# Entry of the MLP: a bank's sum ahead of the next operand's rest, rests of weights sooner, and six sums from VectorE to GpSimd

## The chip, the cores and the metric

One NeuronCore of one Trainium2 chip. The metric is the device time of one execution in microseconds (us). The kernel before took 2927.08 us (median of 3 runs, 2926.19 to 2927.83). TensorE multiplies matrices, VectorE (DVE in the profile), ScalarE (ACT) and GpSimd (POOL) do element-wise work, SyncE (SP) issues most of the DMAs. Each engine executes its own instructions in order and waits on semaphores for the others.

## The reference

One layer of a diffusion transformer, for 256 context tokens and 2048 latent tokens, model width 1024: a modulated RMS norm, one projection, differential attention beside Fourier mixing, an output projection with a gated residual, and then the part that matters here:

```python
xs = xs + g1 * mix
h = rms_norm(xs, norm2_g[l]) * (1 + sc2) + sh2
xs = xs + g2 * sq_relu_mlp(h, w1[l], w2[l])      # square(relu(h @ w1)) @ w2, inner width 4096
```

The same MLP runs for the context tokens `xp`. Everything is float32.

## The kernel before

**Precision.** A float32 product is made of three matmuls on the faster fp32r type. Each operand is split into a high part (ScalarE's cast to fp32r) and a rest (VectorE's `tensor_sub` of operand and high part), and `high*high`, `high*rest` and `rest*high` are summed in PSUM.

**Seven products.** `h @ w1` is done as a 2x2 block product with seven multiplications in place of eight. The 2304 tokens stand in 18 tiles of 128; tile `t` is paired with tile `t + 9`, and the pairs form three token blocks `b` of 384 columns. Seven operands on the token side (`hop[p][b]`, DMAed from a scratch tensor to a tile `hr`, split into `mhh` and `mhl`) meet seven on the weight side. A weight set `q` holds four 128x512 blocks `a11`, `a12`, `a21`, `a22` and four sums of them, `s1` to `s4`; `LEFT` says which one product `p` takes, and its split is `ophW` (high) and `oplW` (rest). Sets 0 to 15 are block 0, and so on.

**The MLP's loop.** `ITEMS` is the order of the products: (q, p) = (0,1), (0,6), (0,2), (0,7), (0,5), (0,4), (1,1), (1,6), (0,3), (1,2), (1,7), (1,5), (1,4), ... The third product of a set stands two places late. One item is 12 matmuls of 128x384 (`mms`, four slices by three parts). Four PSUM banks are used, and products share them: 1 and 2 add up in bank A, 6 and 7 in B, 5 and 3 in C, 4 has D. Between two products of a bank VectorE or ScalarE must read the sum so far: `post` copies A (`us`), makes `u2` and `u3` from B and `us`, and `uz` from C or D. ScalarE turns `uz` into `g` (relu, then square: `squares`), GpSimd sums the `g` (`g_add`), and SyncE stores them.

**Order.** It is written out by hand (`manual_schedule`): the instructions of each engine stand as the Python code issues them. In iteration `n` the loop casts the weights of a later item (`CASTS`, then `n + LEAD + 1`); `w_low` issues the rests of all casts that have none yet; `h_prep` makes high part and rest of a token operand. In the first iterations the token operands of block 0 are still being prepared, in the order 1, 6, 2, 7, 5, 4, 3 (`ORDER`). Their DMA tiles `hr` have three buffers, so the load of operand 7 waits for the rest of operand 1 to be made, 5 for 6, 4 for 2 and 3 for 7.

**The entry.** The out-projection's last tile (17, `LAST`, in two halves `xo17_0` and `xo17_1`) still passes VectorE when the MLP's first operands are prepared: `out_post` multiplies a half's PSUM sum by the gate (`gt`) and adds it to `xo`; `x_store` writes `xo` out. `mlp_ahead` puts the first splits among these steps. The sums of set 0 are made ahead (`w_ahead`; `s4` in `mlp_ahead(2)`, in place in the buffer of `a12`), those of set 1 by `w_add` inside the loop, those of set 2 two items later. Weight blocks have eight buffers (two sets).

Of the kernel before, what the change touches and what calls it, by code (L numbers as in the profile page):

```python
# [41 lines left out]
def body(tc, a, out):  # L42
    nc = tc.nc
    ctx = ExitStack()
    with ctx:
# [1270 lines left out]

        def h_prep(b, p):
            src = HR.pop((b, p))
            pool = hpa if p in (1, 6) else hp[p]
            hi = pool.tile([P, 4, 384], F32R, tag=f"mhh{p}", name=f"mhh{b}_{p}")  # L1320
            lo = pool.tile([P, 4, 384], F32R, tag=f"mhl{p}", name=f"mhl{b}_{p}")
            for c, t in src if isinstance(src, list) else [(slice(0, 4), src)]:
                nc.scalar.copy(hi[:, c, :], t)
                nc.vector.tensor_sub(lo[:, c, :], t, f32(hi[:, c, :]))
            HO[b, p] = hi, lo

        def w_ahead():
# [9 lines left out]
        def mlp_ahead(part):  # L1337

            if part == 0:
                for n in range(2):  # L1340
                    h_prep(0, ORDER[n])
                    w_cast(n)
                    w_low()
                    if n == 0:
                        h_load(0, ORDER[3])
# [14 lines left out]
        with c3o, ExitStack() as c4, ExitStack() as c4x, ExitStack() as c4w:  # L1360
# [67 lines left out]
            def out_post(i, hf):  # L1428
                s = 1 if i < 2 else 0
                gt = t4.tile([P, 512], F32, tag="gt", name=f"gt{i}_{hf}")  # L1430
                nc.vector.tensor_mul(gt, PS.pop((i, hf)), g1[s][:, hf * 512:hf * 512 + 512])
                nc.vector.tensor_add(x_half(i, hf), x_half(i, hf), gt)

# [32 lines left out]
            with tc.manual_schedule():  # L1466
# [42 lines left out]
                for n, i in enumerate(seq[2:], 2):  # L1509
# [6 lines left out]
                    if n == N4 - 1:  # L1516
# [3 lines left out]
                        c5r = ExitStack()  # L1520
                        hpa = c5r.enter_context(tc.tile_pool(name="m_ha", bufs=1, side="right", reuse_waits="tile"))
                    out_post(i, 0)
                    if n == N4 - 1:
                        mlp_ahead(0)
                    finish(seq[n - 1])
# [16 lines left out]
        with c5r, ExitStack() as c5:  # L1542
# [4 lines left out]

            def w_add(q, n):

                R = RAW[q]  # L1550
                x, y, f = (("a21", "a22", nc.vector.tensor_add), ("s1", "a11", nc.vector.tensor_sub),
                           ("a11", "a21", nc.vector.tensor_sub), ("a12", "s2", nc.vector.tensor_sub))[n]
                t = t5.tile([P, 512], F32, tag=f"ws{n}", name=f"ws{n}_{q}", bufs=1)
                f(t, R[x], R[y])
                R[f"s{n + 1}"] = t
# [140 lines left out]
            LAG = []  # L1696
            CASTS = ((), (4,), (5,), (8, 6), (7,), (9,), (10, 11))

            with tc.manual_schedule():
                for n, (q, p) in enumerate(ITEMS):  # L1700
                    b, last = q // NF, q % NF == NF - 1 and q // NF < 2
                    if n < 4:
                        h_prep(0, ORDER[n + 2])
                        if n < 2:
                            h_load(0, ORDER[n + 5])
                    w_low()
                    for c in CASTS[n] if n < len(CASTS) else (n + LEAD + 1,):
                        w_cast(c)
# [5 lines left out]
                    if n == 2:  # L1714
                        mlp_ahead(2)
                    if n == 5:
                        h_prep(0, 3)
                    early = q == 0 and p == 6
                    if early:
                        post(q, p, ps)  # L1720
                    nw = q + 1
                    if q and p == 1 and wset(q) == q:
                        w_add(q, 3)
                    if nw < NQ and wset(nw) == nw:
                        for x in ({7: (0, 1), 5: (2,)} if q == 0 else {6: (0, 1), 2: (2,)}).get(p, ()):
                            w_add(nw, x)
# [235 lines left out]
```

## Time and profile before

| | |
|---|---|
| median of 3 runs | 2927.08 us (2926.19 to 2927.83) |
| the profiled execution, its own time | 2927.01 us |
| its span, first to last instruction | 2925.2 us |
| TensorE busy | 2892.7 us, 99% of the span |
| VectorE, ScalarE, GpSimd busy | 2010.5, 1570.7, 1043.8 us |
| mean granted TensorE clock | 0.998 of full speed |
| MLP's first matmul | 1517.14 us after the span's start |

The timeline views give for each instruction the start, the duration, the engine, the source line, what is written and read, and in brackets how long the engine stood idle before it and who released it. Matmuls are pipelined: each row of 0.34 us starts some 0.17 us after the one before. Buffer numbers are left out of the profile's names, so `mhl` stands for the rest of every token operand and `oplW` for that of every weight operand; the instruction order tells which one it is.

### The profile page before, as it was taken

What the parts mean: (1) busy time and instruction counts of PE and PEld (TensorE: products, weight loads), DVE (VectorE), ACT (ScalarE), POOL (GpSimd) and SP (SyncE); (2) the same over time, 40 slices, a digit from 0 to 9 for tenths busy, and PEclk for the clock granted to TensorE, in tenths of its full rate; (3) what the DMA queues carried; (4) which work ended last, traced back from release to release, by engine and by line L of the source; (5) the groups of instructions that cost most, each with busy time, mean ns of one, the idle gap of its engine ahead of it and who ended that gap; (6) DMA issues with size and microseconds to landing.
All of it is one profiled execution on the core that took longest, in us unless ns stands there. A gap on an engine that the chain in (4) does not pass through costs nothing.

```text
span 2925.2 us, 43918 instructions
## 1 busy us (share of the span) xinstructions
PE 2892.7 (99%) x15497; PEld 2514.0 (86%) x15497; DVE 2010.5 (69%) x3377; ACT 1570.7 (54%) x3535; POOL 1043.8 (36%) x849
## 2 busy tenths in 40 slices
PE   8999999999999999999999999999999999999999
PEld 4888888778888888888889999999998888888887
DVE  6666776788998988974468778777775354345554
ACT  4333323688998989964356556556554322232221
POOL 1111113199898989952213333333332000000000
PEclk9999999999999999999999999999999999999999
DMA  7777878612121211217776667676656454445663
GB/s 279 199 201 190 224 199 260 220 61 76 44 103 43 104 37 44 91 50 214 216 246 208 224 234 235 224 240 221 217 192 229 132 195 150 135 142 176 204 208 108
DMA packets 394414, 495.58 MB, mean 169 GB/s; under 512 B 26403, under 2 KB 307056, under 8 KB 391122
## 3 DMA queue, kind: packets, MB, share of 16 engines
q1 hardware_dynamic: 386560, 477.63, 51.7%
q0 software_dynamic: 2992, 7.28, 0.8%
q10 hardware_dynamic: 4642, 7.88, 0.8%
q8 instruction: 122, 2.00, 0.3%
q14 instruction: 98, 0.80, 0.1%
HBM read 315.20 MB, written 179.57 MB: 169 GB/s over the span
## 4 chain that ended last, share of the span: by engine, by line
PE 93%; ACT 2%; DVE 2%; DMA 1%; POOL 1%; issue 1%; SPq 0%; ACTq 0%; DVEq 0%; POOLq 0%
PE Ss L935 10%; PE ps L87 8%; PE ps L88 8%; PE ps L89 8%; PE pj L88 5%; PE pj L87 5%; PE pj L89 5%; PE pts L990 5%; PE po L87 4%; PE po L89 4%; PE po L88 4%; PE pC L1584 2%; PE pB L1582 2%; PE pB L1584 2%; PE pB L1583 2%; PE pC L1582 2%
## 5 line engine op out<-in xcount | busy, mean ns | idle before, releaser
L940 DVE TENSOR_REDUCE mxs<-Ss 128x1 f32<-128x512 f32 x636 | 413.4, 685 | 66.2 <-PE Ss L935 54.0
L1275 DVE TENSOR_TENSOR sl<-sr,sh 128x768 fp32r<-128x768 f32 x168 | 161.8, 964 | 339.9 <-ACT sh L1274 339.4
L975 POOL TENSOR_TENSOR P0s<-P0s,P1s 128x1024 f32<-128x1024 f32 (+2 forms) x128 | 377.1, 2946 | 10.7
L1274 ACT CAST sh<-sr 128x768 fp32r<-128x768 f32 x168 | 140.2, 835 | 424.9 <-PE ps L88 421.3
L1624 POOL TENSOR_TENSOR gs<-g,g 128x384 f32<-128x384 f32 x48 | 69.7, 1452 | 472.2 <-ACT g L1594 418.2
L959 ACT ACTIVATE P1s<-Ss,mxs 128x512 f32<-128x512 f32 x318 | 215.4, 694 | 36.2 <-DVE mxs L943 34.8
L87 PE MATMUL pj<-wh,hh 128*128 128x512 f32 x576 | 229.4, 398 | 0.7 <-ACT fo L381 0.7
L88 PE MATMUL ps<-tlT,sh 128*128 128x512 f32 x585 | 229.3, 392 | 0.0
L87 PE MATMUL ps<-thT,sh 128*128 128x512 f32 x585 | 229.2, 392 | 0.0
L88 PE MATMUL pj<-wl,hh 128*128 128x512 f32 x576 | 227.9, 396 | 0.5 <-DVE wl L503 0.5
L89 PE MATMUL ps<-thT,sl 128*128 128x512 f32 x585 | 227.7, 389 | 0.0
L89 PE MATMUL pj<-wh,hl 128*128 128x512 f32 x576 | 226.5, 394 | 0.0
L959 ACT ACTIVATE P0s<-Ss,mxs 128x512 f32<-128x512 f32 x318 | 214.3, 691 | 4.6 <-DVE mxs L943 4.0
L935 PE MATMUL Ss<-KS1s,Qs 128*128 128x512 f32 x636 | 196.2, 420 | 5.5 <-ACT P0s L959 3.1
L935 PE MATMUL Ss<-KS0s,Qs 128*128 128x512 f32 x636 | 196.5, 421 | 2.6 <-ACT P1s L959 2.4
L990 PEld LDWEIGHTS pts<-ident,P0s 128*128 128x128 f32 x1280 | 158.3, 140 | 43.0 <-ACT ahs L997 3.3
L990 PE MATMUL pts<-ident,P0s 128*128 128x128 f32 x1280 | 191.3, 273 | 0.7 <-ACT P1s L959 0.7
L1593 ACT ACTIVATE g<-uz 128x384 f32<-128x384 f32 x144 | 75.9, 527 | 203.1 <-DVE uz L1616 172.9
L974 POOL TENSOR_SCALAR P1s<-P1s,tots 128x1024 f32<-128x1024 f32 (+2 forms) x128 | 172.2, 1345 | 5.8
L1002 DVE TENSOR_TENSOR als<-pts,ahs 128x512 fp32r<-128x512 f32 x256 | 165.9, 681 | 6.8 <-ACT ahs L997 6.6
L87 PE MATMUL ps<-ophT,sh 128*128 128x512 f32 x423 | 165.9, 392 | 1.1 <-DVE uz L1616 1.1
L89 PE MATMUL ps<-ophT,sl 128*128 128x512 f32 x423 | 165.7, 392 | 0.0
(622 smaller groups left out, 8230.1 us busy)
## 6 DMA issues: line engine op xcount, KB each, us to landing
sr<-sd SPq DMA_DIRECT2D x84, 768.0 KB, 4.6
a<-in_w SPq DMA_DIRECT2D x184, 256.0 KB, 3.9
sd<-gs SPq DMA_DIRECT2D x192, 192.0 KB, 2.0
sd<-g SPq DMA_DIRECT2D x144, 192.0 KB, 4.4
wm<-in_w_mod SPq DMA_DIRECT2D x32, 512.0 KB, 5.7
Qs<-qd SPq DMA_DIRECT2D x32, 512.0 KB, 3.6
b<-in_w SPq DMA_DIRECT2D x64, 256.0 KB, 5.2
b<-tsum SPq DMA_DIRECT2D x64, 256.0 KB, 4.8
```

The costliest lines, as they stand in the source:

```text
L87: nc.tensor.matmul(ps, lh, rh, start=first, stop=False)
L88: nc.tensor.matmul(ps, lh, rl, start=False, stop=False)
L89: nc.tensor.matmul(ps, ll, rh, start=False, stop=last)
L935: nc.tensor.matmul(S[:, :w], self.Q[:, x, m, j * P:j * P + P], self.hd.KS[m][:, b * 512:b * 512 + w], start=(x == 0), stop=(x == 1))
L940: nc.vector.tensor_reduce(self.mx[j][:, m, b:b + 1], self.S[j, m, b], axis=AX.X, op=ALU.max)
L959: nc.scalar.activation(dst, S, AF.Exp, bias=self.mx[j][:, m, 6:7], accum_out=self.sm[j][:, m, b:b + 1])
L974: nc.gpsimd.tensor_scalar(p, p, tot[:, 3:4], 0.0, op0=ALU.mult, op1=ALU.add)
L975: nc.gpsimd.tensor_add(d, d, p)
L990: nc.tensor.transpose(pt[:, c:c + P], self.p0[j][:, (kb + t) * P:(kb + t + 1) * P], ident)
L1002: nc.vector.tensor_sub(t, self.pt[kb], f32(self.A[kb][0]))
L1274: nc.scalar.copy(hi, src)
L1275: nc.vector.tensor_sub(lo, src, f32(hi))
```

## The change

`mlp_ahead(0)` is split: the first token operand's split is issued before `out_post` of tile 17's first half, the rest of that step after it. Both residual adds of tile 17 (`xo17_0`, `xo17_1`) go from VectorE to GpSimd. `h_prep` becomes `h_parts`, which returns the high part and the rest as two steps; in iteration 1 the rest of operand 7 is issued after `post` of product 6, and with it the load of operand 3. From iteration 2 on, `w_low` runs before the token operand's rest as well. `CASTS` issues the cast for product 3 of set 0 in iteration 5 in place of 3, and `s4` of set 0 is made in iteration 5 in place of 2. All four weight sums of set 1 go to GpSimd, issued in iteration 2 (three of them) and 6 (the fourth). TensorE's and SyncE's orders stay as they are.

```diff
--- before.py
+++ after.py
@@ -1315,14 +1315,27 @@
                 HR[b, p].append((slice(2 * n, 2 * n + 2), f32(t)))
 
         def h_prep(b, p):
+            for half in h_parts(b, p):
+                half()
+
+        def h_parts(b, p):
+
             src = HR.pop((b, p))
             pool = hpa if p in (1, 6) else hp[p]
             hi = pool.tile([P, 4, 384], F32R, tag=f"mhh{p}", name=f"mhh{b}_{p}")
             lo = pool.tile([P, 4, 384], F32R, tag=f"mhl{p}", name=f"mhl{b}_{p}")
-            for c, t in src if isinstance(src, list) else [(slice(0, 4), src)]:
-                nc.scalar.copy(hi[:, c, :], t)
-                nc.vector.tensor_sub(lo[:, c, :], t, f32(hi[:, c, :]))
             HO[b, p] = hi, lo
+            src = src if isinstance(src, list) else [(slice(0, 4), src)]
+
+            def high():
+                for c, t in src:
+                    nc.scalar.copy(hi[:, c, :], t)
+
+            def rest():
+                for c, t in src:
+                    nc.vector.tensor_sub(lo[:, c, :], t, f32(hi[:, c, :]))
+
+            return high, rest
 
         def w_ahead():
 
@@ -1337,8 +1350,11 @@
         def mlp_ahead(part):
 
             if part == 0:
+                h_prep(0, ORDER[0])
+            elif part == 3:
                 for n in range(2):
-                    h_prep(0, ORDER[n])
+                    if n:
+                        h_prep(0, ORDER[n])
                     w_cast(n)
                     w_low()
                     if n == 0:
@@ -1429,7 +1445,7 @@
                 s = 1 if i < 2 else 0
                 gt = t4.tile([P, 512], F32, tag="gt", name=f"gt{i}_{hf}")
                 nc.vector.tensor_mul(gt, PS.pop((i, hf)), g1[s][:, hf * 512:hf * 512 + 512])
-                nc.vector.tensor_add(x_half(i, hf), x_half(i, hf), gt)
+                (nc.gpsimd if i == LAST else nc.vector).tensor_add(x_half(i, hf), x_half(i, hf), gt)
 
             def x_store(i):
                 if i == LAST:
@@ -1519,9 +1535,11 @@
                         ms2 = ctx.enter_context(tc.tile_pool(name="m_s2", bufs=2, side="right", reuse_waits="tile"))
                         c5r = ExitStack()
                         hpa = c5r.enter_context(tc.tile_pool(name="m_ha", bufs=1, side="right", reuse_waits="tile"))
+                    if n == N4 - 1:
+                        mlp_ahead(0)
                     out_post(i, 0)
                     if n == N4 - 1:
-                        mlp_ahead(0)
+                        mlp_ahead(3)
                     finish(seq[n - 1])
                     out_mm(i, 1)
                     if n == N4 - 1:
@@ -1545,11 +1563,12 @@
             pp = c5.enter_context(tc.tile_pool(name="m_p", bufs=2, space=PSUM, reuse_waits="tile"))
             PSB, U, G = {}, {}, {}
 
-            def w_add(q, n):
+            def w_add(q, n, gp=False):
 
                 R = RAW[q]
-                x, y, f = (("a21", "a22", nc.vector.tensor_add), ("s1", "a11", nc.vector.tensor_sub),
-                           ("a11", "a21", nc.vector.tensor_sub), ("a12", "s2", nc.vector.tensor_sub))[n]
+                e = nc.gpsimd if gp else nc.vector
+                x, y, f = (("a21", "a22", e.tensor_add), ("s1", "a11", e.tensor_sub),
+                           ("a11", "a21", e.tensor_sub), ("a12", "s2", e.tensor_sub))[n]
                 t = t5.tile([P, 512], F32, tag=f"ws{n}", name=f"ws{n}_{q}", bufs=1)
                 f(t, R[x], R[y])
                 R[f"s{n + 1}"] = t
@@ -1694,16 +1713,24 @@
 
 
             LAG = []
-            CASTS = ((), (4,), (5,), (8, 6), (7,), (9,), (10, 11))
+            CASTS = ((), (4,), (5,), (6,), (7,), (8, 9), (10, 11))
 
             with tc.manual_schedule():
                 for n, (q, p) in enumerate(ITEMS):
                     b, last = q // NF, q % NF == NF - 1 and q // NF < 2
+                    if n > 1:
+                        w_low()
+                    rest = None
                     if n < 4:
-                        h_prep(0, ORDER[n + 2])
-                        if n < 2:
+                        high, rest = h_parts(0, ORDER[n + 2])
+                        high()
+                        if n != 1:
+                            rest()
+                        if n < 1:
                             h_load(0, ORDER[n + 5])
                     w_low()
+                    if n == 5:
+                        mlp_ahead(2)
                     for c in CASTS[n] if n < len(CASTS) else (n + LEAD + 1,):
                         w_cast(c)
                     squares()
@@ -1712,17 +1739,20 @@
                     if fn:
                         fn(*args)
                     if n == 2:
-                        mlp_ahead(2)
+                        for x in range(3):
+                            w_add(1, x, True)
                     if n == 5:
                         h_prep(0, 3)
                     early = q == 0 and p == 6
                     if early:
                         post(q, p, ps)
+                        rest()
+                        h_load(0, ORDER[6])
                     nw = q + 1
                     if q and p == 1 and wset(q) == q:
-                        w_add(q, 3)
-                    if nw < NQ and wset(nw) == nw:
-                        for x in ({7: (0, 1), 5: (2,)} if q == 0 else {6: (0, 1), 2: (2,)}).get(p, ()):
+                        w_add(q, 3, q == 1)
+                    if q and nw < NQ and wset(nw) == nw:
+                        for x in {6: (0, 1), 2: (2,)}.get(p, ()):
                             w_add(nw, x)
                     if p == (7 if q else 5) and q + 2 < NQ and wset(q + 2) == q + 2:
                         w_load(q + 2)
```

What stands in the engines' orders at three places. First VectorE from the gating of tile 17's second half (`gt17_1`) to the rest of token operand 4 (`mhl0_4`); `mhl0_p` is the rest of token operand p of block 0, `oplW0_p` that of the weight operand of product p in set 0, `u2_0` the sum that reads bank B after product 6. Before:

```order
L1431 TENSOR_TENSOR gt17_1_17333<-po4_17_1_17300,g1_0_15293 128x512
L1432 TENSOR_TENSOR xo17_1_17042<-xo17_1_17042,gt17_1_17333 128x512
L1324 TENSOR_TENSOR mhl0_2_17370<-hr0_2_17001,mhh0_2_17369 128x1536
L1306 TENSOR_TENSOR oplW0_2_17328<-a12_0_16664,ophW0_2_17327 128x512
L1306 TENSOR_TENSOR oplW0_7_17331<-a21_0_16666,ophW0_7_17330 128x512
L1324 TENSOR_TENSOR mhl0_7_17393<-hr0_7_17269,mhh0_7_17392 128x1536
L1606 TENSOR_TENSOR u2_0_17414<-pB0_17401,us_0_17390 128x384
L1324 TENSOR_TENSOR mhl0_5_17417<-hr0_5_17325,mhh0_5_17416 128x1536
L1306 TENSOR_TENSOR oplW0_5_17399<-wsa1_17104,ophW0_5_17398 128x512
L1352 TENSOR_TENSOR a12_0_16664<-a12_0_16664,wsa2_17105 128x512
L1324 TENSOR_TENSOR mhl0_4_17438<-hr0_4_17373,mhh0_4_17437 128x1536
L1306 TENSOR_TENSOR oplW0_4_17422<-a22_0_16668,ophW0_4_17421 128x512
```

With the change:

```order
L1447 TENSOR_TENSOR gt17_1_17333<-po4_17_1_17300,g1_0_15293 128x512
L1336 TENSOR_TENSOR mhl0_2_17370<-hr0_2_17001,mhh0_2_17369 128x1536
L1306 TENSOR_TENSOR oplW0_2_17328<-a12_0_16664,ophW0_2_17327 128x512
L1306 TENSOR_TENSOR oplW0_7_17331<-a21_0_16666,ophW0_7_17330 128x512
L1625 TENSOR_TENSOR u2_0_17411<-pB0_17398,us_0_17390 128x384
L1336 TENSOR_TENSOR mhl0_7_17393<-hr0_7_17269,mhh0_7_17392 128x1536
L1306 TENSOR_TENSOR oplW0_5_17396<-wsa1_17104,ophW0_5_17395 128x512
L1336 TENSOR_TENSOR mhl0_5_17418<-hr0_5_17325,mhh0_5_17417 128x1536
L1306 TENSOR_TENSOR oplW0_4_17422<-a22_0_16668,ophW0_4_17421 128x512
L1336 TENSOR_TENSOR mhl0_4_17444<-hr0_4_17373,mhh0_4_17443 128x1536
```

The add `xo17_1` and the sum into `a12_0` (that is `s4`) are gone from here, `u2_0` stands ahead of `mhl0_7`, and `oplW0_4`, `oplW0_5` ahead of the token rests `mhl0_4`, `mhl0_5`.

Second GpSimd, from the last norm's power (`nrsb8`) to the first sum of `g`. Before:

```order
L84 TENSOR_TENSOR nrsb8_17222<-nssb8_17219,mhalf_178 128x1
L1624 TENSOR_TENSOR gs0_0_17621<-g12_0_17601,g22_0_17503 128x384
L84 TENSOR_TENSOR fss_15268<-fss_15268,mhalf_178 128x1
L1626 TENSOR_TENSOR gs1_0_17655<-gs0_0_17621,g11_0_17448 128x384
L1628 TENSOR_TENSOR gs2_0_17676<-g11_0_17448,g12_0_17601 128x384
```

With the change (`ws0_1` to `ws3_1` are the four weight sums of set 1):

```order
L84 TENSOR_TENSOR nrsb8_17222<-nssb8_17219,mhalf_178 128x1
L1448 TENSOR_TENSOR xo17_0_17041<-xo17_0_17041,gt17_0_17262 128x512
L1448 TENSOR_TENSOR xo17_1_17042<-xo17_1_17042,gt17_1_17333 128x512
L1573 TENSOR_TENSOR ws0_1_17436<-a21_1_17113,a22_1_17115 128x512
L1573 TENSOR_TENSOR ws1_1_17438<-ws0_1_17436,a11_1_17109 128x512
L1573 TENSOR_TENSOR ws2_1_17440<-a11_1_17109,a21_1_17113 128x512
L1573 TENSOR_TENSOR ws3_1_17548<-a12_1_17111,ws1_1_17438 128x512
L1643 TENSOR_TENSOR gs0_0_17621<-g12_0_17601,g22_0_17502 128x384
```

Six 128x512 adds now stand between the two, where nothing stood.

Third ScalarE, from the high part of token operand 4 (`mhh0_4`) to that of operand 3 (`mhh0_3`); `ophW0_3` is the high part of the weight operand for product 3, a cast of `s4`. Before:

```order
L1323 CAST mhh0_4_17437<-hr0_4_17373 128x1536
L1300 CAST ophW0_3_17442<-a12_0_16664 128x512
L1300 CAST ophW1_1_17445<-a11_1_17109 128x512
L1593 ACTIVATE g11_0_17448<-pA0_17377 128x384
L1594 ACTIVATE g11_0_17448<-g11_0_17448 128x384
L1300 CAST ophW1_6_17471<-ws1_1_17465 128x512
L1300 CAST ophW1_2_17500<-a12_1_17111 128x512
L1593 ACTIVATE g22_0_17503<-uz_0_17497 128x384
L1594 ACTIVATE g22_0_17503<-g22_0_17503 128x384
L1323 CAST mhh0_3_17519<-hr0_3_17396 128x1536
```

With the change:

```order
L1332 CAST mhh0_4_17443<-hr0_4_17373 128x1536
L1300 CAST ophW1_1_17447<-a11_1_17109 128x512
L1612 ACTIVATE g11_0_17450<-pA0_17377 128x384
L1613 ACTIVATE g11_0_17450<-g11_0_17450 128x384
L1300 CAST ophW1_6_17468<-ws1_1_17438 128x512
L1300 CAST ophW0_3_17496<-a12_0_16664 128x512
L1300 CAST ophW1_2_17499<-a12_1_17111 128x512
L1612 ACTIVATE g22_0_17502<-uz_0_17492 128x384
L1613 ACTIVATE g22_0_17502<-g22_0_17502 128x384
L1332 CAST mhh0_3_17518<-hr0_3_17414 128x1536
```

`ophW0_3` has moved behind `ophW1_6` and stands just ahead of `ophW1_2`, the two passes on `g22_0` and `mhh0_3`; on VectorE its rest `oplW0_3` now comes after `mhl0_3` and the `uz` of product 4 (before, it came ahead of both).

## Rows read from the trace of the kernel before

**Rows 1.** The page: engine, busy us (share of the span), instructions.

```profile
PE 2892.7 (99%) x15497; PEld 2514.0 (86%) x15497; DVE 2010.5 (69%) x3377; ACT 1570.7 (54%) x3535; POOL 1043.8 (36%) x849
```

**Rows 2.** Busy time by stretch: stretch, length, busy (instructions) per engine, PEclk, DMA share, GB/s.

```profile
1517.10:1545.00 27.90, 24.51 (x133) 22.57 (x132) 24.98 (x33) 17.28 (x27) 0.00 (x0) 1.00 0.66 224
...
1600.00:1700.00 100.00, 100.00 (x578) 100.00 (x577) 76.48 (x122) 57.94 (x112) 34.41 (x28) 1.00 0.68 222
```

**Rows 3.** TensorE in order of time at the MLP entry: start us, us, instruction, [idle before].

```profile
1517.14 0.34 PE L1582 MATMUL pA<-mhh,ophW 128*128 128x384 f32 x1
...
1524.42 0.41 PE L1582 MATMUL pB<-mhh,ophW 128*128 128x384 f32 x1 [0.85 <-ACT ophW L1300]
...
1532.77 0.44 PE L1584 MATMUL pA<-mhh,oplW 128*128 128x384 f32 x1 [0.65 <-DVE oplW L1306]
...
1538.12 0.44 PE L1583 MATMUL pC<-mhl,ophW 128*128 128x384 f32 x1 [1.07 <-DVE mhl L1324]
1538.40 0.34 PE L1584 MATMUL pC<-mhh,oplW 128*128 128x384 f32 x1
...
1542.91 0.44 PE L1582 MATMUL pB<-mhh,ophW 128*128 128x384 f32 x1 [0.50 <-DVE u L1606]
```

**Rows 4.** VectorE in order of time, same stretch, same columns.

```profile
1517.34 0.69 DVE L1431 TENSOR_TENSOR gt<-po,g 128x512 f32<-128x512 f32 x1 [0.41 <-PE po L89]
1518.06 0.69 DVE L1432 TENSOR_TENSOR xo<-xo,gt 128x512 f32<-128x512 f32 x1
1518.67 1.75 DVE L1324 TENSOR_TENSOR mhl<-hr,mhh 128x1536 fp32r<-128x1536 f32 x1
1520.34 1.29 DVE L1306 TENSOR_TENSOR oplW<-a,ophW 128x512 fp32r<-128x512 f32 x2
1522.05 1.76 DVE L1324 TENSOR_TENSOR mhl<-hr,mhh 128x1536 fp32r<-128x1536 f32 x1 [0.42 <-ACT mhh L1323]
1523.72 0.55 DVE L1606 TENSOR_TENSOR u<-pB,us 128x384 f32<-128x384 f32 x1
...
1527.36 1.76 DVE L1324 TENSOR_TENSOR mhl<-hr,mhh 128x1536 fp32r<-128x1536 f32 x1 [0.21 <-ACT mhh L1323]
...
1542.31 0.55 DVE L1606 TENSOR_TENSOR u<-pB,us 128x384 f32<-128x384 f32 x1
```

**Rows 5.** ScalarE in order of time, same stretch, same columns.

```profile
1520.54 1.48 ACT L1323 CAST mhh<-hr 128x1536 fp32r<-128x1536 f32 x1 [0.61 <-DVE mhl L1324]
...
1534.81 1.46 ACT L1323 CAST mhh<-hr 128x1536 fp32r<-128x1536 f32 x1
```

**Rows 6.** The chain that ended last, in order of time: start us, us, what.

```profile
1520.45 5.37 DMA hr<-hd
```

**Rows 7.** VectorE and GpSimd, last tiles of the out-projection, in order of time.

```profile
1502.33 1.07 DVE L1432 TENSOR_TENSOR xo<-xo,gt 128x512 f32<-128x512 f32 x1
...
1502.92 1.62 POOL L1460 TENSOR_TENSOR ht<-hTb,ht 128x512 f32<-128x512 f32 x1
```

**Rows 8.** VectorE and GpSimd, change of token block inside the MLP, in order of time.

```profile
1749.74 1.76 DVE L1324 TENSOR_TENSOR mhl<-hr,mhh 128x1536 fp32r<-128x1536 f32 x1 [0.85 <-ACT mhh L1323]
...
1749.84 2.53 POOL L1626 TENSOR_TENSOR gs<-gs,g 128x384 f32<-128x384 f32 x1
...
1751.88 1.04 DVE L1306 TENSOR_TENSOR oplW<-ws,ophW 128x512 fp32r<-128x512 f32 x1
...
1752.34 1.47 POOL L1628 TENSOR_TENSOR gs<-g,g 128x384 f32<-128x384 f32 x1
...
1753.38 2.05 DVE L1324 TENSOR_TENSOR mhl<-hr,mhh 128x1536 fp32r<-128x1536 f32 x1
```

**Rows 9.** TensorE near the start of the kernel, in order of time.

```profile
37.91 1.33 PE L494 MATMUL pta<-ident,x 128*128 128x128 f32 x5 [2.18 <-DVE hTa L479]
```

**Rows 10.** Busy time by stretch near the start, columns as in rows 2.

```profile
38.00:39.00 1.00, 1.00 (x5) 1.00 (x6) 0.96 (x2) 1.00 (x3) 0.00 (x0) 0.50 0.49 197
...
44.00:45.00 1.00, 1.00 (x5) 0.87 (x4) 1.00 (x3) 1.00 (x3) 0.00 (x0) 0.87 0.91 279
```

## The prediction

> **What bounds the kernel now.** I read the page first: TensorE is busy 99% of the span [rows 1], so the change can pay only where TensorE waits, and next the windows by stage. From 1600 to 1700 us TensorE is never idle and begins 578 matmuls in 100 us, one per 0.173 us; from 1517.1 to 1545 us, the MLP's entry, it is busy 24.51 of 27.90 us [rows 2]. The timeline of TensorE shows the waits there: for the high part of an operand (and, by the program, for the sum that reads bank B), for a weight's rest, for a token's rest, for `u` [rows 3]; three shorter ones stand between. Between 1517.14 and 1542.91 lie ten items of 12 matmuls, 120 x 0.173 = 20.8 us of work in 25.8 us: 5.0 us are lost, 0.17% of the kernel. That is the most that could be won here.
>
> Who is late? VectorE is busy 24.98 of the 27.90 us [rows 2], and its timeline explains each wait [rows 4]. `u2_0` (bank B) could have run at 1521.5, when product 6 ended, but stands behind the rest of operand 7 and ends at 1524.27; TensorE begins product 7 at 1524.42. The rest of operand 4 ends at 1529.12, and from there to the third matmul of product 3 at 1538.40 VectorE and ScalarE pass work to each other without a long pause: 9.3 us. `u2_1` ends at 1542.86, product 7 of set 1 begins at 1542.91. So VectorE sets the entry's pace.
>
> **The change part by part, without GpSimd's side.** The token rests cost VectorE 1.67 us from start to next start (1522.05 to 1523.72), the 512-wide rests 0.60 (two in 1.29, the second overlapping the first), `u` 0.47 [rows 4].
>
> The first operand's rest ahead of `gt17_0`, and `xo17_0` taken off, lie before 1517.34, where VectorE waits 0.41 us for TensorE anyway [rows 4]: worth nothing to TensorE. (GpSimd's `xo17_0` may hold operand 6's rest by a turn, worked out below at 1.1 us; the step then ends near 1517.0, still inside that wait. Without this cover `gt17_1` would be late by what is over.) Operand 7's load starts some 1.7 us sooner, but nothing below waits for it.
>
> From `gt17_1` on, in the new order: operand 2's rest needs no `xo17_1` ahead of it and starts at 1517.96, two weight rests follow, VectorE is free at 1520.8. `u2_0` waits for product 6, 1521.53 to 1522.05. Operand 7's high part ends at 1522.02 [rows 5], its rest runs from 1522.05 as before. Then `oplW0_5`, operand 5, `oplW0_4`, operand 4: 0.60 + 1.67 + 0.60 + 1.75 after 1523.72 is 1528.35. Before it was 1529.12 [rows 4]; saved 0.8.
>
> The way from there to product 3's third matmul has new members: `u3_0`, `oplW1_1`, `uz`, `oplW1_6`, `s4` on VectorE (2.8 us), then on ScalarE `ophW0_3`, which now waits for `s4`, and behind it `ophW1_2`, two passes of `g22` and operand 3's high part (3.6 with 1.46 for the last [rows 5]), then operand 3's rest, `uz`, `oplW0_3` on VectorE (2.9): 9.2 us, as long as before. So what TensorE wins ahead of product 3 it loses there, in two waits (operand's rest, then weight's rest) where there was one. Behind it VectorE has four instructions less; `u2_1` no longer comes late, and its wait goes (0.50 us idle [rows 3], about 0.66 against the cadence). Sum of this side: 0.8 + 0.66 = 1.5 us won.
>
> **GpSimd's side.** Does a sum on GpSimd cost VectorE nothing? The trace answers. At 1749 us VectorE makes token rests while GpSimd sums `g` [rows 8]. GpSimd's add issued at 1749.84 ends at 1752.37, 0.87 after VectorE's rest (1751.50); VectorE's next rest, issued at 1751.88, ends 0.55 after that; GpSimd's next add ends at 1753.81, 0.89 after VectorE's; the token rest issued at 1753.38 ends at 1755.43, 1.62 after GpSimd's. The two take strict turns: an instruction with two SBUF inputs on one engine waits out the other's. `u`, which reads PSUM, stands between these rows unhindered. Tile adds show the price for 512 columns: `xo` issued at 1502.33 ends at 1503.40, GpSimd's add at 1504.54, 1.14 later [rows 7]. A 512-wide turn in a busy VectorE stream therefore takes 1.14 + 0.55 for a rest in place of 0.60, and 1.14 + 1.62 for a token rest in place of 1.67: 1.1 us each.
>
> The Trainium skill says the same of the two engines (GPSIMD Engine Reference, § 8 Key points): GpSimd shares its SBUF interfaces with VectorE and contends with VectorE's instructions that have two SBUF inputs. It gives no duration; without the rule the sum would be 1.5 us won, with it and the trace's turns it is what follows.
>
> Nothing holds the four weight sums back: their blocks have long landed, so GpSimd starts them right behind `xo17_1`, which waits for `gt17_1` (1518.03). Five turns fall where VectorE is the pace: `xo17_1` behind operand 2's rest, `ws0_1` behind `oplW0_2`, `ws1_1` behind `oplW0_7` (half of it beside `u2_0`, which needs no turn), `ws2_1` behind operand 7, `ws3_1` behind `oplW0_5`. That is 4 x 1.1 + 0.6 = 5.0 us, of which 0.7 vanish in the wait that `u2_0` had for product 6. Operand 4's rest then ends at 1528.35 + 5.0 - 0.7 = 1532.6, 3.5 later than before; product 3's third matmul comes at 1532.6 + 9.2 = 1541.8. Product 7 of set 1 follows 22 matmul starts later (3.8 us), as TensorE no longer waits for `u2_1`, at 1545.7: **2.8 us later than before**. From there the orders are the same.
>
> Bounds of this term: no turn at all gives the gain of 1.5; five turns at the whole 1.62 of GpSimd's row [rows 7], which holds its own wait for VectorE too, with nothing absorbed, are 8.1 and put operand 4's rest at 1536.4 and the end 6.7 later, 2933.7. I take the worked-out value, since the rows of 1749 show the very same instruction kinds in the same state.
>
> **Other waits added.** SyncE: `xo17_1`'s store waits for GpSimd's add (1520.9 in place of 1518.8); behind it stand the loads of operands 4 and 3 and of set 2's blocks. Operand 4's load goes out near 1521.4 in place of 1520.45; with 5.37 us to landing [rows 6] and 1.5 for its high part it is ready by 1528.4, ahead of VectorE's turn for it at 1530.9. Operand 3's load leaves 2 us later, with 6 to spare. Set 2's blocks no longer wait for `oplW0_3`, they come sooner.
>
> **Rivals.** (1) GpSimd's sums cost nothing: they slip into gaps that VectorE has, or the turns are shorter than in rows 7 and 8. Then the entry wins 1.5: 2925.5 us. Against it: VectorE has less than 3 us of gaps in 27.9 [rows 2], most of them at waits for ScalarE. (2) Slower by more: the granted clock falls. At 37.91 TensorE, after sparse work, had waited 2.18 us [rows 9]; from 38 us on the granted clock was 0.50, the 1.2 GHz level, until past 44 us [rows 10]. All waits of rows 3, 1.07 at most, left it at 1.00 [rows 2]. With the turns TensorE waits 2.0 us before operand 7's rest, 2.1 before operand 5's, and near 2.8 in three pieces around product 3. A fall after the first two is mostly hidden, as TensorE waits at product 3 anyway; one at product 3 slows some 6.5 us of work to half speed, 3.3 us more: 6.1 in all, 2933.1. It decides from the point where a fall costs 3 us in the open. (3) All waits go: 2922.0; it would need VectorE to finish product 3's operands 3 us sooner than its row of work allows. (4) The moved steps cancel: 2927.
>
> **Numbers.** The profiled execution took 2927.01 us, 0.07 under the median of the runs; I add the sum to it: 2927.0 + 2.8 = 2929.8. Chances: the turns as worked out 0.62, rival 1 0.17, rival 2 0.14 (half of it beyond the bound below), rival 3 0.02, rival 4 0.05. A measurement here tells 0.2%, 5.9 us, from no change; 2921.1 would be faster, 2932.9 slower. The waits at the entry sum to less than that, so faster is left 0.02; slower gets 0.08 from rival 2 and the upper bound of the turns; the rest, 0.90, is within. The range takes in rival 1 and most of rival 2: 2925.4 to 2932.8; the turns alone reach from 2928.6 to 2931.6.
>
> **What the changed profile would show.** GpSimd: `xo` and four `ws` in a row from 1519.6 to about 1528.7, some 1.3 to 2.8 us each, back to back with VectorE. VectorE: weight rests of 1.8 us and token rests over 2.3 in that stretch, `u2` at about 1523 (right: 1521.5 would mean no turns). TensorE: the wait at product 7 for operand 7's rest, a longer one for operand 5's, two at product 3, none for `u2_1`, product 7 of set 1 at 1545.7. Wrong if `ws` rows take 1.3 us each and VectorE's rests beside them stay at 0.69 and 1.75, or if PEclk under 1.00 stands in a window of the entry.

## The result and the profile after

The changed kernel takes **2930.14 us** (median of 22 runs, 2928.48 to 2932.61), the kernel before 2926.43 (22 runs, 2925.10 to 2931.29). The ratio is 1.0012, with a 95% interval of 1.0006 to 1.0017: 3.7 us slower, less than the 0.2% that the prediction called measurable, but told apart from no change. The forecast was 2929.8.

The profiled execution, the longest of the 22, has a span of 2930.8 us, 5.6 more than before. Not all of that is the change's: the MLP's first matmul begins at 1519.02 in place of 1517.14, and over the twelve profiled executions of this case that point lies anywhere from 1515.7 to 1519.2. I count from this matmul, M, on. From M to the end of the span before took 2925.2 - 1517.14 = 1408.06 us, the changed kernel 1411.78: **3.72 us** more, what the medians say too. Behind the last tile's transposes (M + 39.7 before, M + 43.4 with the change) the rest of the span takes 1368.33 to 1368.43 us in all twelve traces, so what differs between the kernels arises ahead of that point.

The page's row of the engines, for [rows 1]:

```profile
PE 2894.8 (99%) x15497; PEld 2516.6 (86%) x15497; DVE 2010.0 (69%) x3371; ACT 1570.2 (54%) x3535; POOL 1056.4 (36%) x855
```

GpSimd has six instructions more and VectorE six less; TensorE's busy time grows by 2.1 us with the same number of matmuls, a sign that some ran slower. VectorE in order of time at the entry, for [rows 4]:

```profile
1515.35 2.70 DVE L1336 TENSOR_TENSOR mhl<-hr,mhh 128x1536 fp32r<-128x1536 f32 x1
...
1519.22 0.69 DVE L1447 TENSOR_TENSOR gt<-po,g 128x512 f32<-128x512 f32 x1 [0.57 <-PE po L89]
...
1521.49 3.51 DVE L1306 TENSOR_TENSOR oplW<-a,ophW 128x512 fp32r<-128x512 f32 x2
1524.92 0.55 DVE L1625 TENSOR_TENSOR u<-pB,us 128x384 f32<-128x384 f32 x1
1525.39 2.37 DVE L1336 TENSOR_TENSOR mhl<-hr,mhh 128x1536 fp32r<-128x1536 f32 x1
1527.68 1.77 DVE L1306 TENSOR_TENSOR oplW<-wsa,ophW 128x512 fp32r<-128x512 f32 x1
1529.37 2.83 DVE L1336 TENSOR_TENSOR mhl<-hr,mhh 128x1536 fp32r<-128x1536 f32 x1
...
1532.73 1.75 DVE L1336 TENSOR_TENSOR mhl<-hr,mhh 128x1536 fp32r<-128x1536 f32 x1
...
1536.53 0.68 DVE L1368 TENSOR_TENSOR a<-a,wsa 128x512 f32<-128x512 f32 x1
1540.77 1.76 DVE L1336 TENSOR_TENSOR mhl<-hr,mhh 128x1536 fp32r<-128x1536 f32 x1 [3.56 <-ACT mhh L1332]
```

GpSimd in the same stretch:

```profile
1519.99 2.76 POOL L1448 TENSOR_TENSOR xo<-xo,gt 128x512 f32<-128x512 f32 x1 [3.55 <-DVE gt L1447]
1522.68 1.76 POOL L1573 TENSOR_TENSOR ws<-a,a 128x512 f32<-128x512 f32 x1
1524.52 1.62 POOL L1573 TENSOR_TENSOR ws<-ws,a 128x512 f32<-128x512 f32 x1
1526.10 2.80 POOL L1573 TENSOR_TENSOR ws<-a,a 128x512 f32<-128x512 f32 x1
1528.86 1.72 POOL L1573 TENSOR_TENSOR ws<-a,ws 128x512 f32<-128x512 f32 x1
```

The two lists interlock. Two weight rests at 1521.49 take 3.51 us in place of 1.29, the token rests at 1525.39 and 1529.37 2.37 and 2.83 in place of 1.75, the weight rest between them 1.77 in place of 0.68: 2.22 + 0.62 + 1.08 + 1.09 = 5.0 us, in the stretch in which GpSimd's five adds lie. From 1532.7 on, behind the last of them, the same instructions take 1.75 and 0.68 again. `u` (1524.92), which reads PSUM, is not slowed.

TensorE, for [rows 3]:

```profile
1519.02 0.34 PE L1601 MATMUL pA<-mhh,ophW 128*128 128x384 f32 x1
...
1525.61 0.41 PE L1601 MATMUL pB<-mhh,ophW 128*128 128x384 f32 x1 [0.17 <-DVE u L1625]
1527.81 0.44 PE L1602 MATMUL pB<-mhl,ophW 128*128 128x384 f32 x1 [1.79 <-DVE mhl L1336]
...
1532.26 0.45 PE L1602 MATMUL pC<-mhl,ophW 128*128 128x384 f32 x1 [2.10 <-DVE mhl L1336]
...
1542.58 0.44 PE L1602 MATMUL pC<-mhl,ophW 128*128 128x384 f32 x1 [1.35 <-DVE mhl L1336]
1543.64 0.44 PE L1603 MATMUL pC<-mhh,oplW 128*128 128x384 f32 x1 [0.63 <-DVE oplW L1306]
...
1549.13 0.34 PE L1601 MATMUL pB<-mhh,ophW 128*128 128x384 f32 x1
```

It waits 0.17 and 1.79 us at product 7 and 2.10 at operand 5's rest, then reaches product 3 and waits there twice: 1.35 for the operand's rest, 0.63 for the weight's. What made these two late stands on ScalarE, for [rows 5]:

```profile
1537.24 1.14 ACT L1300 CAST ophW<-a 128x512 fp32r<-128x512 f32 x2 [5.55 <-DVE a L1368]
...
1539.27 1.46 ACT L1332 CAST mhh<-hr 128x1536 fp32r<-128x1536 f32 x1
```

ScalarE stood 5.55 us in front of the cast of the sum `s4` (VectorE, 1536.53), and operand 3's high part (1539.27) is queued behind it. VectorE in turn waits 3.56 us for that high part (1540.77). Behind the two waits the granted clock fell; windows, for [rows 2], with TensorE's columns alone (stretch, length, busy us and matmuls, granted clock, DMA share, GB/s):

```profile
1544.00:1545.00 1.00, 1.00 (x6) 0.63 0.10 26
1545.00:1546.00 1.00, 1.00 (x5) 0.50 0.68 217
...
1547.00:1548.00 1.00, 1.00 (x6) 0.66 0.77 227
```

From about 1544.3 to 1547.7 TensorE had 0.50, its 1.2 GHz level, and the matmuls begin 0.32 us apart in place of 0.173. Product 7 of set 1 begins at 1549.13, M + 30.11; before it was M + 25.77.

### The profile page after: what moved, and what is told of

Same layout as the page of the kernel before. It is cut to its first block, busy times and chain, and to the rows that moved or that the text cites. A ratio compares the mean times of both kernels' runs of the same rounds, so it can differ in the third digit from the quotient of the medians.

```text
span 2930.8 us, 43925 instructions
## 1 busy us (share of the span) xinstructions
PE 2894.8 (99%) x15497; PEld 2516.6 (86%) x15497; DVE 2010.0 (69%) x3371; ACT 1570.2 (54%) x3535; POOL 1056.4 (36%) x855
## 4 chain that ended last, share of the span: by engine, by line
PE 89%; POOL 3%; ACT 2%; DVE 2%; DMA 2%; issue 1%; SPq 0%; ACTq 0%; POOLq 0%; DVEq 0%
PE Ss L935 9%; PE ps L87 8%; PE ps L88 8%; PE ps L89 8%; PE pj L87 4%; PE pj L88 4%; PE pj L89 4%; PE pts L990 4%; PE po L87 3%; PE po L89 3%; PE po L88 3%; PE pC L1603 2%; PE pC L1601 2%; PE pC L1602 2%; PE pA L1601 2%; PE pA L1602 2%
```

## The experiments

The theory to test: turns between GpSimd and VectorE set the loss. Rivals: the moved steps lose it without GpSimd, by the late sum `s4`; the fall of the clock does. Times are medians; "by trace" is the time from M to the end of the span less the 1408.06 of before. The third matmul of product 3 and product 7 of set 1 are counted from M.

| run | product 3, 3rd | product 7, set 1 | by trace | median less before | ratio, 95% interval |
|---|---|---|---|---|---|
| before | 21.26 | 25.77 | 0 | 0 | |
| changed | 24.62 | 30.11 | +3.72 | +3.71 | 1.0012 (1.0006 to 1.0017) |
| e1_no_sums | 20.89 | 26.38 | +0.01 | +0.45 | 1.0001 (0.9992 to 1.0009) |
| e2_sums_twice | 28.08 | 33.56 | +7.22 | +7.49 | 1.0027 (1.0017 to 1.0036) |
| e3_fill | 24.64 | 28.57 | +2.64 | +3.42 | 1.0012 (1.0003 to 1.0021) |
| e4_gpsimd_alone | 22.79 | 26.75 | +1.05 | +1.68 | 1.0004 (0.9995 to 1.0013) |
| e5_vector_sums | 23.50 | 28.75 | +2.41 | +3.70 | 1.0014 (1.0005 to 1.0022) |
| e6_high_early | 19.34 | 23.21 | -2.56 | -1.83 | 0.9994 (0.9985 to 1.0003) |
| e7_sum4_early | 22.83 | 26.78 | +1.08 | +1.47 | 1.0006 (0.9997 to 1.0014) |
| e8_high_early_gp | 22.06 | 25.87 | -0.51 | +0.17 | 1.0001 (0.9992 to 1.0010) |
| e9_vector_order | 18.40 | 23.52 | -2.26 | -1.42 | 0.9994 (0.9985 to 1.0002) |
| e10_sum4_late | 23.22 | 29.84 | +3.44 | +3.49 | 1.0012 (1.0003 to 1.0021) |

An interval here is some 2.5 us wide to either side, as wide as most of these differences; the offsets in the traces decide, one execution for each run, and the medians follow them within 1.3 us.

**e1_no_sums**, the four sums of set 1 left out.

```diff
-                        for x in range(3):
-                            w_add(1, x, True)
+                        RAW[1].update(s1=RAW[1]["a21"], s2=RAW[1]["a22"], s3=RAW[1]["a21"], s4=RAW[1]["a12"])
...
-                        w_add(q, 3, q == 1)
+                        if q > 1:
+                            w_add(q, 3)
```

> The changed kernel with the four weight sums of set 1 left out (their places in the products are taken by the blocks themselves, so products 3, 5, 6 and 7 of set 1 multiply other numbers of the same shape). Of the five turns only the tile add's stays. Theory of turns: operand 4's rest ends 0.4 later than the sum without GpSimd's side gave, 11.7 us after the MLP's first matmul (15.5 in the changed kernel, 12.0 before); weight rests there take 0.7 us in place of 1.8, token rests 1.75; no fall of the clock; the time is near 2925.4 us, 4.7 under the changed kernel and 1 under the kernel before (range 2924.6 to 2926.4). Rival, the moved steps lose the time by themselves (late sum of operand 3's weight, two waits at product 3): operand 4's rest may come sooner, but the time stays within 1 us of the changed kernel's 2930.1.

VectorE's rests are short again but for the one pair that meets `xo17_1`, 1.1 us over:

```profile
1519.80 2.41 DVE L1306 TENSOR_TENSOR oplW<-a,ophW 128x512 fp32r<-128x512 f32 x2
...
1522.61 1.74 DVE L1336 TENSOR_TENSOR mhl<-hr,mhh 128x1536 fp32r<-128x1536 f32 x1
1524.27 0.68 DVE L1306 TENSOR_TENSOR oplW<-wsa,ophW 128x512 fp32r<-128x512 f32 x1
```

Without the sums 3.7 us are gone by trace (4.7 forecast). But the run did not come below the kernel before (median 2926.76, above the range that was stated): product 3's third matmul is 0.37 sooner, at M + 20.89, and product 7 of set 1 still 0.61 later. Between them 22 starts at 0.173 make 3.8 us and took 5.49: TensorE waited twice at product 3 (1.79 and 1.07 us from start to start), and the clock fell. The moved steps bring a fall of the clock without any of the four sums on GpSimd; of its adds only the last tile's are left.

**e2_sums_twice**, each of the four sums made twice.

```diff
-                f(t, R[x], R[y])
+                for _ in range(2 if gp else 1):
+                    f(t, R[x], R[y])
```

> The changed kernel with each of set 1's four sums made twice on GpSimd into the same tile, the same numbers. Theory of turns: four more turns of 1.1 us while VectorE is the pace, 4.4 us later at product 3, near 2934.5 us (2933.0 to 2937, the upper end if the clock falls for longer); the extra sums show 1.6 to 2.8 us each. Rival, the moved steps alone: GpSimd has 19 us of nothing behind its sums, so the time stays at 2930.1 (2929.3 to 2931).

VectorE and GpSimd behind the changed kernel's last turn:

```profile
1529.36 1.77 DVE L1306 TENSOR_TENSOR oplW<-a,ophW 128x512 fp32r<-128x512 f32 x1
...
1531.05 2.83 DVE L1336 TENSOR_TENSOR mhl<-hr,mhh 128x1536 fp32r<-128x1536 f32 x1
...
1532.23 4.49 POOL L1574 TENSOR_TENSOR ws<-a,ws 128x512 f32<-128x512 f32 x2
...
1534.27 1.30 DVE L1306 TENSOR_TENSOR oplW<-a,ophW 128x512 fp32r<-128x512 f32 x1
```

Two more full turns (1.77 in place of 0.68, 2.83 in place of 1.75) and two of 0.62 (weight rests of 1.30, the second at 1535.96): 3.4 us, and product 3's third matmul comes 3.46 later than in the changed kernel. Turns confirmed, at 0.9 a sum on the mean; the rival that the moved steps alone make the loss is out. The clock fell twice here, to 0.50 from 1535 to 1538 behind a wait at product 4 and once more behind product 3.

**e3_fill**, eight matmuls in front of product 3.

```diff
+                    if n == 8:
+                        fill = pp.tile([P, 384], F32, tag="pD", name="pfill")
+                        for k in range(8):
+                            nc.tensor.matmul(fill, WO5[1, 6][0][:, 0:P], HO[0, 6][0][:, 0, :], start=k == 0, stop=k == 7, skip_group_check=True)
                     ps = mms(q, p)
```

> The changed kernel with eight matmuls more ahead of product 3 of set 0, into a spare buffer of bank D that nobody reads: TensorE works through 1.4 us of what was a wait of 1.35 us for operand 3's rest. Theory that the clock's fall at product 3 costs 1.5 us of the 3.7: the granted clock stays at 1.00 (windows of 1 us behind product 3 show no 0.50), near 2928.5 us (2928.0 to 2929.2). Rival, the fall follows from all the waits of the entry together or costs nothing in the open: clock 0.50 again, 2930.1 or up to 0.3 more.

TensorE around product 3, and its windows there and, ahead of them, at product 7:

```profile
1539.51 1.55 PE L1740 MATMUL pfill<-mhh,ophW 128*128 128x384 f32 x8
...
1541.37 0.44 PE L1602 MATMUL pC<-mhl,ophW 128*128 128x384 f32 x1
1542.44 0.45 PE L1603 MATMUL pC<-mhh,oplW 128*128 128x384 f32 x1 [0.63 <-DVE oplW L1306]
```

```profile
1527.00:1528.00 1.00, 1.00 (x4) 0.50 0.41 74
...
1542.00:1545.00 3.00, 2.56 (x15) 1.00 0.30 90
```

The third matmul stands where it stood, M + 24.64, the clock stays at 1.00 behind it, and product 7 of set 1 comes 1.54 sooner. That is the clock's share in these two traces; 0.46 of it is given back where the last tile's transposes wait for their operand. The median fell by 0.3 alone, to 2929.73, inside its interval and above the range that was stated. Unexpected: in this execution the clock had fallen at product 7 (0.50 at 1527), where the changed kernel's waits, equal within 0.01 us, left it at 1.00. It cost nothing, since TensorE then had to wait for operand 5 anyway, 0.89 in place of 2.44 us from start to start.

**e4_gpsimd_alone**, the kernel before with GpSimd's adds and sums alone.

```diff
-                nc.vector.tensor_add(x_half(i, hf), x_half(i, hf), gt)
+                (nc.gpsimd if i == LAST else nc.vector).tensor_add(x_half(i, hf), x_half(i, hf), gt)
...
                     if n == 2:
                         mlp_ahead(2)
+                        for x in range(3):
+                            w_add(1, x, True)
...
-                        w_add(q, 3)
+                        w_add(q, 3, q == 1)
...
```

> The kernel before with only GpSimd's part of the change: the last tile's two adds and set 1's four sums on GpSimd, the order of all else as before. Theory of turns: operand 4's rest ends 15.5 us after the MLP's first matmul in place of 12.0, but VectorE is then rid of four sums and the sum of operand 3's weight is early, so product 3 comes 1.7 late and product 7 of set 1 about 1.0 late: 2927.4 us (2926.6 to 2929.0, the upper end with a fall of the clock). If GpSimd's sums cost VectorE nothing: 1.9 under the kernel before, 2924.5.

By trace +1.05, and operand 4's rest ends at M + 15.44: as the turns said. The interval of the medians does not tell it from no change. The biggest wait moved to product 7. Behind it the clock fell (0.53 from 1527 to 1530.5), but TensorE still had to wait for operand 4's rest after that (0.40 us from start to start), so the fall cost little in the open:

```profile
1527.35 0.66 PE L1583 MATMUL pB<-mhh,ophW 128*128 128x384 f32 x1 [2.92 <-DVE u L1607]
```

**e5_vector_sums**, the changed kernel's moved steps with all sums on VectorE.

```diff
-                (nc.gpsimd if i == LAST else nc.vector).tensor_add(x_half(i, hf), x_half(i, hf), gt)
+                nc.vector.tensor_add(x_half(i, hf), x_half(i, hf), gt)
...
-                        for x in range(3):
-                            w_add(1, x, True)
...
-                        w_add(q, 3, q == 1)
+                        w_add(q, 3)
...
```

> The changed kernel with the last tile's adds and set 1's sums on VectorE again, at the places that they had before; the moved steps stay moved. By the rows of VectorE: operand 4's rest 11.3 us after the MLP's first matmul (12.0 before), then the way to product 3's third matmul with two 0.65 us sums and one of 0.6 on it, 11.1 us in place of 9.2: product 3's third matmul 0.6 to 1.2 us later than before, the time 2927.5 us (2926.6 to 2928.5). Theory of turns: 2 to 3 us under the changed kernel. Rival, the moved steps cost all of the 3.7: 2930.

A miss: the median is as far above before as the changed kernel's, so GpSimd is not needed for a loss of this size: the rival came. ScalarE here stands in front of `s4`'s cast too, and VectorE for operand 3's high part:

```profile
1529.87 1.76 DVE L1336 TENSOR_TENSOR mhl<-hr,mhh 128x1536 fp32r<-128x1536 f32 x1 [1.10 <-ACT mhh L1332]
...
1535.61 0.69 DVE L1368 TENSOR_TENSOR a<-a,wsa 128x512 f32<-128x512 f32 x1
...
1536.34 1.14 ACT L1300 CAST ophW<-a 128x512 fp32r<-128x512 f32 x2 [2.72 <-DVE a L1368]
...
1538.36 1.45 ACT L1332 CAST mhh<-hr 128x1536 fp32r<-128x1536 f32 x1
...
1539.85 1.76 DVE L1336 TENSOR_TENSOR mhl<-hr,mhh 128x1536 fp32r<-128x1536 f32 x1 [3.55 <-ACT mhh L1332]
```

The high part could not begin until 2.75 us after the sum began (1535.61 to 1538.36); the forecast also left out 1.10 us that VectorE waits at 1529.87 for operand 4's high part, whose load ScalarE waited for. That wait is the whole of the miss at product 3's third matmul (M + 23.50 against 22.4 at most); the clock's fall behind it is the rest.

**e10_sum4_late**, the kernel before with the late sum and its casts alone, and **e7_sum4_early**, the changed kernel with that one step put back.

```diff
-            CASTS = ((), (4,), (5,), (8, 6), (7,), (9,), (10, 11))
+            CASTS = ((), (4,), (5,), (6,), (7,), (8, 9), (10, 11))
...
-                    if n == 2:
-                        mlp_ahead(2)
...
                     w_low()
+                    if n == 5:
+                        mlp_ahead(2)
```

(e7 is the reverse, in the changed kernel.)

> The kernel before, all sums on VectorE, with the late sum alone: the fourth weight sum of set 0 and the casts of the weights behind it are issued where the changed kernel has them. Theory (the late sum costs by ScalarE's row): operand 3's high part ends 37.2 - 33.7 = 3.5 us behind the sum, product 3's third matmul comes 1.6 later than before in two waits; with a fall of the clock behind them 1.5 more, less 0.8 of the wait for u that goes: 1 to 3 slower than the kernel before, 2928.5 us (2927.4 to 2930). Rival (the sum's place costs nothing, the loss in the run with all moved steps and no GpSimd came from the other steps): 2926.4.

> The changed kernel with one step put back: the fourth weight sum of set 0 and the cast of product 3's weight that waits for it are issued where the kernel before had them; GpSimd's sums and all else stay. Theory (the late sum holds up ScalarE, which makes operand 3's high part behind it, so product 3 waits twice and the clock falls): one wait at product 3 of under 1 us, third matmul there near 22.5 us after the MLP's first matmul (24.6 in the changed kernel), granted clock 1.00 behind it, product 7 of set 1 at 26.3 (30.1), 0.5 given back in the last tile's transposes: 3.3 under the changed kernel, 2926.9 us (2926.2 to 2928.3). Rival (GpSimd's turns are all of the loss): 0.6 more of VectorE's work ahead of operand 4, 2930 or more.

ScalarE in e10, then TensorE's windows there:

```profile
1535.92 1.14 ACT L1300 CAST ophW<-a 128x512 fp32r<-128x512 f32 x2 [2.72 <-DVE a L1352]
...
1537.95 1.45 ACT L1323 CAST mhh<-hr 128x1536 fp32r<-128x1536 f32 x1
```

```profile
1540.00:1542.00 2.00, 0.56 (x1) 0.86 0.00 0
...
1546.00:1547.00 1.00, 1.00 (x5) 0.50 0.96 274
...
1548.00:1549.00 1.00, 1.00 (x7) 0.88 0.55 158
```

This step alone gives +3.44, nearly all that the whole change gives: product 3's third matmul 1.96 later, then 2.8 us to the clock (1.5 forecast), which stayed at 0.50 until past 1548 here. Put back (e7), with GpSimd's turns left in, product 3 waits 0.15 us, the clock stays at 1.00, and +1.08 is left, what e4 has. TensorE at product 3 in e7, without an idle stretch:

```profile
1538.40 0.45 PE L1602 MATMUL pC<-mhl,ophW 128*128 128x384 f32 x1
```

At product 3's third matmul the two parts add up: 1.96 (e10) and 1.53 (e4) make 3.49, the changed kernel has 3.36; its other moved steps stand in neither. Behind it they do not: the way from there to product 7 took 6.62 us in e10, with the longer fall, and 5.49 in the changed kernel.

**e8_high_early_gp**, the changed kernel with operand 3's high part ahead of the cast that waits for `s4`.

```diff
                     if n == 5:
+                        high, rest3 = h_parts(0, 3)
+                        high()
                         mlp_ahead(2)
...
-                        h_prep(0, 3)
+                        rest3()
```

> The changed kernel with one step moved: ScalarE makes operand 3's high part ahead of the weight cast that waits for the late sum, in the 5.5 us in which it waited for that sum. GpSimd's sums and the late sum stay. Theory (product 3 is late by ScalarE's row and not by VectorE's): operand 3's rest follows the sum on VectorE at once, product 3's third matmul comes near 22.1 us after the MLP's first, no fall of the clock, 3.7 under the changed kernel, 2926.4 us (2925.8 to 2927.6), while the weight rests of 1.8 us and token rests of 2.4 to 2.8 us beside GpSimd's sums stay as they were. Rival (the turns decide all): 2930.

VectorE's turns as in the changed kernel, and operand 3's rest (1535.47) straight behind the sum:

```profile
1519.82 3.51 DVE L1306 TENSOR_TENSOR oplW<-a,ophW 128x512 fp32r<-128x512 f32 x2
...
1527.70 2.85 DVE L1336 TENSOR_TENSOR mhl<-hr,mhh 128x1536 fp32r<-128x1536 f32 x1
...
1535.47 1.75 DVE L1336 TENSOR_TENSOR mhl<-hr,mhh 128x1536 fp32r<-128x1536 f32 x1
```

One cast moved on ScalarE gives back the whole loss, by trace and by median, with five turns and a late sum still there: product 3's third matmul comes 2.56 sooner than in the changed kernel and no fall follows it.

**e6_high_early** and **e9_vector_order**, versions without GpSimd: e6 is the kernel before with the high part early and `u` of product 6 ahead of operand 7's rest.

```diff
...
+                    if n == 4:
+                        high, rest3 = h_parts(0, 3)
+                        high()
...
-                        h_prep(0, 3)
+                        rest3()
...
                         post(q, p, ps)
+                        rest()
```

e9 is e6 with the steps that its expectation names; besides, it issues the cast for product 3 in iteration 4 in place of 3.

> The kernel before, all sums on VectorE, with two steps moved: u of product 6 goes ahead of operand 7's rest, and ScalarE makes operand 3's high part behind the squares of the first product, ahead of the weight cast that waits for a sum, in place of behind the squares of the fifth. The rows give: product 7 begins 0.6 us sooner, VectorE has no wait of 1.9 us for operand 3's high part, product 3 waits 1 us less, product 7 of set 1 has no wait for u: 2.0 us under the kernel before, 2924.4 us (2923.8 to 2925.6). Rival: the next step on VectorE (operand 4's rest, or the sums) is late in its place and it gains under 0.7 us, 2925.8 or more.

> All sums on VectorE, operand 3's high part early and u of product 6 ahead of operand 7's rest (as in the run that had these two steps alone), and besides each weight's rest in the entry ahead of the token rest behind it, set 1's first two sums and the fourth sum of set 0 behind the rest of set 1's first weight. That run's waits at product 4 (0.4 us for a weight's rest) and at product 1 of set 1 (0.8) go: 1.0 less than there, product 7 of set 1 at 22.2 us after the MLP's first matmul in place of 23.2, 3.5 under the kernel before by the trace, 2923.5 us (2922.5 to 2925). Rival: VectorE's row is full, the waits turn up at product 3 and product 7 instead, and it ends within 0.3 of that run.

e6 has operand 3's rest without a wait, and TensorE at 1.00 through the entry. By trace it is 2.56 under the kernel before, and 2.05 under e8, so the turns and the late sum, with the other steps in which the two differ, still cost e8 something that its moved cast pays for. The ratio's interval still reaches 1. In e9 the waits named did go (0.4 and 0.8 at product 4 and product 1), but one of 0.94 came at product 2 of set 1, for ScalarE's copy `us`, queued behind casts that waited for the third sum. The rival's size came, 0.3 from e6 by trace, at another place than it named. Operand 3's rest in e6, then the wait in e9:

```profile
1532.31 1.75 DVE L1336 TENSOR_TENSOR mhl<-hr,mhh 128x1536 fp32r<-128x1536 f32 x1
```

```profile
1538.54 0.44 PE L1595 MATMUL pA<-mhh,ophW 128*128 128x384 f32 x1 [0.94 <-ACT us L1617]
```

## Why the prediction came out right, and where it did not

**Right, by rows.** Operand 6's rest met `xo17_0` (2.70 us) and `gt17_1` still waited for TensorE (0.57): no loss there. `u2_0` begins at M + 5.90, five turns cost 5.0 us (forecast 5.0), operand 4's rest ends 3.48 later than before (forecast 3.5), and from there to product 3's third matmul it is 9.16 us (forecast 9.2). GpSimd's rows end where they were expected (M + 11.6), 1.6 to 2.8 us each, and `u2_1`'s wait is gone. The Trainium skill's rule of the shared SBUF interfaces (GPSIMD Engine Reference, § 8 Key points) agrees with e1 and e2, which give it a price of 0.9 us a 512-wide sum in this stream.

**The step that failed: "Product 7 of set 1 follows 22 matmul starts later (3.8 us)".** It took 5.49, at half clock for some 3.4 us: rival 2's mechanism, given 0.14, at half of its 3.3 us. It came at the place it named, product 3, and in e1, e5 and e10, with no sum of set 1 on GpSimd, too. The prediction saw the two waits there and reckoned them "as long as before", a cost of nothing; it compared the way's length and left what the clock does behind two such waits to a rival. A PEclk under 1.00 in a window of the entry was one of the prediction's own signs of being wrong, and it came (0.50 from 1544.3). The second miss, "From there the orders are the same", went the other way: before, the last tile's transposes waited 0.28 us for their operand, and in the changed kernel they do not, some 0.6 in all with the matmuls around them. So +4.34 at product 7 became +3.72. The wait before:

```profile
1551.81 0.55 PE L1664 MATMUL ptf<-ident,xnf 128*128 128x128 f32 x3 [0.28 <-DVE xnf L1655]
```

**Why the number held.** 2.8 was forecast and 3.7 came; the base, one execution at 2927.0, was 0.6 above the median of 22 runs. That is luck: it covered most of the 0.9 us by which the sum fell short. (The sum's upper bound is off by a little: by its own steps five turns of 1.62 end 6.5 us later, not 6.7. Nothing came near it.)

**The attribution failed more than the sum.** The prediction booked the moved steps as 1.5 won and GpSimd as the whole loss. Either part alone loses: by trace GpSimd's +1.05 (e4), the moved steps with all sums on VectorE +2.41 (e5), the late sum alone +3.44 (e10). Even without any sum of set 1 (e1) the moved steps win nothing: 0.37 at product 3's third matmul, taken back by the clock. The place of most of the loss is the queue behind ScalarE's wait for `s4`, which the prediction listed member by member and took for a given length: with the sum put back +1.08 is left (e7), and e8, which moves one member, is back at the time of before. (That member was late in the kernel before too: there VectorE waited 1.92 us for it, and e6, which moves it and one `u`, is 2.56 under it by trace.) How far the fall of the clock is worth its 1.5 us in the medians stays open: e3's trace shows it, e3's median does not resolve it. Of the other executions there is only the mean granted clock to three places, which a fall of 3.4 us moves by 0.0006. It was 0.997 or less in 12 of the 22 of the changed kernel, in 5 of the 11 of e3 and in 1 of 85 of the kernel before; so the falls are not of the profiled execution alone, but where each came is not shown.

## What to carry to other kernels

Moving an add to an engine that idles is not free if both engines read two SBUF operands without pause: look in the trace for stretched rows of the busy one (here 0.68 to 1.77 us). Where a step is moved later, list what is queued behind the instruction that waits for it on the other engine; one cast that does not depend on it, put ahead, gave back the whole loss (e8). And price two waits close together at TensorE by what the granted clock does behind them, not by their sum.

## What the hardware showed unexpectedly

In the one trace that each run has, half clock behind two waits at product 3 (1.55 to 1.80 and 1.06 to 1.07 us from start to start) came in all five runs that had both (changed, e1, e2, e5, e10). In e5 and e10 a third wait of 2.03 us stood ahead, and the clock fell before the wait of 1.07 was over. The half clock lasted 3.4 us, 6.8 in e10; with one of the waits shortened and eight matmuls in its place (e3) it did not come. At product 7 the same waits, within 0.01 us (0.17 to 0.18 and 1.78 to 1.79 us idle), left 1.00 in the changed kernel, e2 and e7, and brought 0.50 in e3 and e8: a wait's length alone did not decide it there. A GpSimd turn's price is not fixed: 1.1 us in most rows, 0.62 in the rows that stand behind an instruction that reads PSUM and needs no turn (`mhl` of 2.37 behind `u` in the changed kernel, `oplW` of 1.30 in e2).
